# Two layers of a diffusion backbone on one core: expert rows in 8 KB runs, a smaller descriptor memory for GpSimd, one more load tile and two more work tiles

## The chip, the core and the metric

The kernel runs on one core of a Trainium2 chip. Its engines are PE (TensorE: matmuls and their weight loads), DVE (VectorE), ACT (ScalarE), POOL (GpSimd) and SP (SyncE, which here issues loads and stores). Sixteen DMA engines move data between HBM and the core's SBUF, which has 128 partitions. Matmul results land in PSUM. The metric is the device time of one launch in microseconds (us); the kernel before has a median of 1786.24 us over 3 runs (1786.08 to 1787.52).

## The reference

All data are fp32. There are 256 latent tokens and 256 context tokens of width 1024 and two layers; in the second the context tokens are only read. In short:

```python
for l in range(2):
    sh1, sc1, g1, sh2, sc2, g2 = split(silu(c) @ w_mod[l] + b_mod[l])   # and the same for c_ctx
    u = h * (1 + sc1) + sh1
    y = four_mixers_gated_and_projected(u, w_in[l], w_branch[l], w_out[l])
    h = layer_norm(ALPHA * h + g1 * y, ln1)
    u = h * (1 + sc2) + sh2                                # latent and context tokens apart
    aff = softmax(u @ w_router[l])                         # 16 experts
    for e in range(16):                                    # each expert takes its 32 best tokens
        idx = top_k(aff[:, e], 32)
        a, v = u[idx] @ w_gate[l, e], u[idx] @ w_up[l, e]  # 1024 x 1024 each
        out[idx] += aff[idx, e] * ((silu(a) * v) @ w_down[l, e])
    h = layer_norm(ALPHA * h + g2 * out, ln2)
```

One expert has three matrices of 4 MB. Layer 0 runs them for 64 rows (32 latent, 32 context), layer 1 for 32.

## The kernel before

**Stages.** Each layer has the modulation vectors, the projections and mixers (lines to about 860), the routing (`route`, `choose`), and then the experts in order 0 to 15 (`gu0`, `down0` in layer 0 and `gu1`, `down1` in layer 1), each with SwiGLU between the two parts. Tokens of an expert are gathered by a matmul with a one-hot matrix (`gather`, `gather_one`), turned so that the width lies on partitions (transposes of PE against an identity, which put the tile to be turned in the weight load), and modulated into `xs`. In `down0` and `down1` the activations are turned in the same way (L1100, L1127). An expert's matmul then takes 128 indices of the contracted dimension at a time: step `kt` has on partition p the index kt * 128 + p, and the weight tile must hold the same row there.

**Loads of the experts.** `ex_raw` cuts a matrix into four 1 MB parts of 256 rows. A part lies in a tile of [128, 2, 1024]: partition p gets row p and row 128 + p, thus two runs of 4 KB. Where a part goes into a pair of tiles of [128, 1024] (tags `b4`, `p`, `pt`) or four of [128, 512] (`wbs`), `go` issues one load for each tile. The last expert's `w_down` is cut by columns instead, into runs of 1 KB.

**What sets the order of the loads.** The loop at the end of `trunk` issues all loads from SP in the order in which the program needs them, up to `LEAD` = 16 parts ahead. SP works in order: where the next tile is still in use, it and all behind it wait. Which tile a part gets is written in three tables: `early` (tiles that are free while the last mixer runs), `order` (the tiles as they come free at the end of the mixers), and `ring` (the cycle afterwards). Tags: `raw` (4 tiles of 8 KB a partition, also used for all weights of the mixers), `w8` (7), `q8`, `k8`, `cst`, `wbr` (1 each), the pairs and `wbs`. Smaller work tiles (2 KB a partition) have the tag `t2`, 7 of them. PE, DVE and ACT are ordered by the language's scheduler; SP and POOL keep the written order.

**GpSimd's loads.** POOL issues the small ones: `b_mod` (`load_b`), the layer norm vectors (`load_ln`, `ln_rows`), `w_router`, the bias table (L510). A part of SBUF, 16 KB of each partition, is set aside for the descriptors that these loads are made of.

**Where the contracted index order enters.** It is in `modT` and `lnT` (vectors with the width on partitions), in `wr` (the router), in the transposes of `turned` (L902), `gather` (L1010), `gather_one` (L1036), `down0` (L1100) and `down1` (L1127), and, undone, in `g_bcast` (L321, L324), which turns a vector of `modT` into rows.

Of the kernel before, what the change touches and what calls it, by code (L numbers as in the profile page):

```python
# [86 lines left out]
def trunk(ctx: ExitStack, tc: tile.TileContext, x, c, ctx_in, c_ctx, w_mod, b_mod, w_in, qk_gain,  # L87
          sink_logit, na_rpb, w_branch, w_out, ln1_g, ln1_b, w_router, w_gate, w_up, w_down,
          ln2_g, ln2_b, consts, ident_in, out):
    nc = tc.nc  # L90
# [5 lines left out]

    N_RAW, N_W8, N_T2 = 4, 7, 7
    N4 = {"b4": 10, "p": 2, "pt": 2}
# [72 lines left out]
    def load_b(l):  # L171
        bsrc = t2([48, 128])
        G.dma_start(bsrc, b_mod[l].rearrange("(k p) -> k p", p=128))
        p = ps_t([128, 48])
        T.transpose(p, bsrc, ident[0:48, 0:48])
        V.tensor_copy(bT[l], p)

    def load_ln(l):
        lsrc = t2([32, 128])
        for n, v in enumerate((ln1_g, ln1_b, ln2_g, ln2_b)):  # L180
            G.dma_start(lsrc[8 * n:8 * n + 8], v[l].rearrange("(k p) -> k p", p=128))
        p = ps_t([128, 32])
        T.transpose(p, lsrc, ident[0:32, 0:32])
        V.tensor_copy(lnT[l].rearrange("p n k -> p (n k)"), p)

# [57 lines left out]
    def mod_tr(l, group):  # L243

        grp, n = group[0] // 4, len(group)
        step = group[1] - group[0]
        qs = slice(group[0] % 4, group[-1] % 4 + 1, step)
        p = ps_t([128, 4, 8])
        for g in range(4):
            T.matmul(p[:, g], mrows[l, group][:, g * 128:g * 128 + 128], sel[:, 0:8], start=True, stop=True)  # L250
        mt = modT[l][:, 4 * grp:4 * grp + 4][:, qs]
        V.tensor_tensor(mt, p.rearrange("p g (q j) -> p q g j", j=2)[:, qs],
                        bT[l][:, grp * 16:grp * 16 + 16].rearrange("p (q g) -> p q g", g=4)[:, qs].unsqueeze(3)
                        .to_broadcast([128, n, 4, 2]), op=OP.add)
# [60 lines left out]
    def g_bcast(l, m, j, ns=range(2)):  # L315
        t = gbc[l, m, j] if (l, m, j) in gbc else b4([128, D])
        gbc[l, m, j] = t
        for n in ns:
            p = ps_mm()
            for g in range(4):  # L320
                T.matmul(p[:, g * 128:g * 128 + 128],  # L321
                         modT[l][:, 2 * m + n, g, j:j + 1].to_broadcast([128, 128]), ident,
                         start=True, stop=True)
            A.activation(t[:, n * 512:n * 512 + 512], p, AF.Copy)  # L324

# [33 lines left out]
    def ex_raw(l, e, kind, q):  # L359
# [7 lines left out]

        rows = w[l, e, q * 256:q * 256 + 256, :].rearrange("(k p) n -> p k n", p=128)

        def go(t):  # L370
            if isinstance(t, list):
                n = 2 * D // len(t)
                for k in range(len(t)):
                    nc.sync.dma_start(t[k], rows[:, k * n // D, k * n % D:k * n % D + n])
            else:
                nc.sync.dma_start(t, rows)
        return (("ex", l, e, kind, q), [128, 2, D], go)
# [66 lines left out]
    def small_loads(l):  # L444
# [7 lines left out]
        G.memset(wr[:, end:end + 1], 0.0)  # L452
        G.dma_start(wr[:, 0:8], w_router[l].rearrange("(k p) e -> p k e", p=128))
        st_["small"] = {"gq": gq, "snk": snk, "wr": wr}

    def layer(l):
# [440 lines left out]
        def turned(t, hf):  # L897
# [3 lines left out]
            for k in range(4):  # L901
                T.transpose(pt[:, k], st_["h"][t][:, (4 * hf + k) * 128:(4 * hf + k) * 128 + 128], ident)  # L902
            (A.activation(u, pt, AF.Copy) if hf else V.tensor_copy(u, pt))
# [90 lines left out]
        def gather(gr, s, pr):  # L994
# [14 lines left out]
            for q in range(4):  # L1009
                T.transpose(p[:, q].rearrange("p n e c -> p (n e c)"), rows[:, q * 128:q * 128 + 128], ident)  # L1010
            for n in range(2):
# [9 lines left out]
        def gather_one(s, e):  # L1021
# [75 lines left out]
        def down0(e, a):  # L1097
            p = ps_t([128, 4, 128])
            for q in range(4):
                T.transpose(p[:, q], a[:, q * 128:q * 128 + 128], ident)  # L1100
            hT = t2([128, 4, 128])
# [22 lines left out]
        def down1(e, a):  # L1124
            p = ps_t([128, 4, 64])
            for q in range(4):
                T.transpose(p[:, q], a[:, q * 128:q * 128 + 128], ident[0:64, 0:64])  # L1127
            hT = t2([128, 4, 64])
# [539 lines left out]
    def ex_tile(tag, shape):  # L1668
# [6 lines left out]
        if tag == "wbs":  # L1675
# [5 lines left out]
    flat = [(j, r) for j, (fn, rs) in enumerate(events) for r in rs]  # L1681
    order = [["raw"] * 2 + ["wbr", "wbs"] + ["b4"] * 2 + ["raw"] * 2 + ["w8"] * 3 + ["q8", "b4"] + ["w8"] * 4 + ["k8", "cst"]
             + ["raw"] * 2 + ["wbr", "b4", "b4", "raw"],
                    ["b4"] * 2 + ["raw"] * 4 + ["wbs", "wbr"] + ["w8"] * 2 + ["b4"] + ["w8"] * 3 + ["q8"]]
    ring = [["raw"] + ["w8"] * 3 + ["q8"] + ["w8"] * 4 + ["cst"] + ["raw"] * 2 + ["wbr", "raw"],
            ["cst"] + ["w8"] * 2 + ["raw"] * 2 + ["p", "pt"] + ["raw"] * 2 + ["wbr"] + ["w8"] * 5 + ["q8"]]
    early = [deque(["cst"]), deque(["cst", "w8", "w8", "k8", "p", "pt"])]
# [59 lines left out]
```

## Time and profile before

| what | value |
|---|---|
| median of 3 runs | 1786.24 us (1786.08 to 1787.52) |
| the profiled execution | 1786.01 us, of which 1783.9 us from its first to its last instruction |
| PE busy, matmuls | 1556.6 us, 87% |
| DVE, ACT, POOL busy | 39%, 24%, 7% |
| moved by DMA | 533.04 MB in 194120 packets, mean 299 GB/s |
| mean granted TensorE clock | 0.954 |

The kernel is one program with stages of different limits, so the shares above are averages. The stages are told apart by the line of GB/s in 40 slices of 44.6 us each and by windows. A packet is one contiguous run that a DMA engine moves; the count of packets and the MB of a stretch give its mean run. PE's busy time counts from the start of a matmul to its modelled end.

### The profile page before, as it was taken

How to read it: one execution, taken by the hardware profiler on the slowest of the kernel's cores; microseconds unless marked ns; L12 is line 12 of the kernel's file. 1: busy time of each engine (PE TensorE's matmuls, PEld its weight loads, DVE VectorE, ACT ScalarE, POOL GpSimd, SP SyncE). 2: the span in 40 equal slices, each digit the busy share in tenths (PEclk: the TensorE clock that was granted, in tenths of full speed). 3: DMA queues.
4: the chain of work that ended last, by engine and by line, in shares of the span. 5: the costliest groups of instructions: out<-in, count | busy, mean ns of one | idle time of the engine just before them, and what ended most of it. 6: DMA issues, size and time to landing. Idle time of an engine off the chain costs nothing.

```text
span 1783.9 us, 22960 instructions
## 1 busy us (share of the span) xinstructions
PE 1556.6 (87%) x9315; PEld 891.8 (50%) x9315; DVE 700.0 (39%) x1378; ACT 432.7 (24%) x929; POOL 131.6 (7%) x176
## 2 busy tenths in 40 slices
PE   7999999999989989899998899999977666767665
PEld 4777778778854333323332588888832212112112
DVE  3564463663542332222222685857533101112114
ACT  2343433343231010101200454445321001001000
POOL 1200012111010000000000320111100000000000
PEclk9999999999989999999999999999979889888888
DMA  9544354453659999999999665657889999999996
GB/s 310 169 145 175 113 182 109 145 185 122 259 194 375 395 409 409 409 409 409 409 409 400 230 236 174 226 120 262 327 312 408 409 409 409 409 409 409 409 409 243
DMA packets 194120, 533.04 MB, mean 299 GB/s; under 512 B 9520, under 2 KB 61088, under 8 KB 194016
## 3 DMA queue, kind: packets, MB, share of 16 engines
q1 hardware_dynamic: 192016, 527.49, 77.8%
q0 software_dynamic: 1856, 4.02, 1.3%
q8 instruction: 73, 1.20, 0.3%
q14 instruction: 31, 0.25, 0.0%
q10 hardware_dynamic: 144, 0.07, 0.0%
HBM read 530.50 MB, written 1.05 MB: 298 GB/s over the span
## 4 chain that ended last, share of the span: by engine, by line
PE 66%; DMA 15%; issue 11%; DVE 5%; ACT 2%; POOL 1%; SPq 0%; ACTq 0%; DVEq 0%; POOLq 0%
PE mm L769 14%; PE mm L1086 12%; PE mm L531 7%; DMA w<-in_w_up_dram 6%; PE mm L1107 5%; DMA raw<-in_w_up_dram 4%; PE mm L780 3%; PE mm L1120 2%; PE pt L217 2%; PE mm L849 2%; DMA w<-in_w_down_dram 2%; PE ps L1003 2%; PE ps L641 2%; PE pt L722 1%; PE ps L1144 1%
## 5 line engine op out<-in xcount | busy, mean ns | idle before, releaser
L769 PE MATMUL mm<-w,b 128*128 128x512 f32 (+1 forms) x1536 | 291.1, 341 | 0.4 <-DVE b L424 0.4
L769 PEld LDWEIGHTS mm<-w,b 128*128 128x128 f32 x1536 | 238.1, 189 | 46.2 <-issue 15.9
L1075 ACT ACTIVATE t<-mm 128x512 f32<-128x512 f32 (+1 forms) x32 | 19.0, 594 | 666.2 <-PE mm L1120 354.7
L1076 DVE SCALAR_TENSOR_TENSOR t<-t,mm 128x512 f32<-128x512 f32 (+1 forms) x32 | 21.9, 683 | 368.3 <-ACT t L1075 368.3
L424 DVE TENSOR_TENSOR b<-raw,b 128x1024 fp32r<-128x1024 f32 (+1 forms) x95 | 113.2, 1194 | 118.3 <-ACT b L422 113.6
L531 PE MATMUL mm<-b,w 128*128 128x512 f32 (+1 forms) x720 | 148.7, 359 | 5.2 <-ACT b L422 3.6
L531 PEld LDWEIGHTS mm<-b,w 128*128 128x128 f32 x720 | 115.7, 192 | 30.6 <-ACT b L422 4.0
L422 ACT ACTIVATE b<-raw 128x1024 fp32r<-128x1024 f32 (+1 forms) x96 | 97.9, 1021 | 126.0 <-PE mm L769 90.3
L1093 DVE TENSOR_TENSOR k<-mm,b 32x512 f32<-32x512 f32 (+1 forms) x96 | 53.1, 553 | 184.8 <-PE mm L1107 84.7
L1120 PE MATMUL mm<-w,b 128*32 128x512 f32 x416 | 92.3, 725 | 30.5 <-DMA w<-in_w_up_dram 25.6
L1086 PE MATMUL mm<-w,b 128*64 128x512 f32 x480 | 116.9, 596 | 1.9 <-DMA w<-in_w_gate_dram 1.2
L798 POOL TENSOR_TENSOR b<-b,t 128x256 f32<-128x256 f32 x72 | 56.2, 794 | 502.5 <-DVE t L792 485.6
L780 PE MATMUL mm<-w,wbs 128*128 128x512 f32 (+1 forms) x384 | 78.4, 339 | 0.1
L1120 PE MATMUL mm<-raw,b 128*32 128x512 f32 x256 | 49.2, 664 | 31.1 <-DMA raw<-in_w_up_dram 17.4
L1086 PEld LDWEIGHTS mm<-w,b 128*64 128x64 f32 x480 | 37.9, 137 | 70.1 <-issue 63.9
L1086 PE MATMUL mm<-raw,b 128*64 128x512 f32 x280 | 70.9, 594 | 0.7 <-DMA raw<-in_w_gate_dram 0.7
L780 PEld LDWEIGHTS mm<-w,wbs 128*128 128x128 f32 x384 | 61.2, 188 | 8.8 <-ACT w L630 0.3
L1120 PEld LDWEIGHTS mm<-w,b 128*32 128x32 f32 x416 | 17.3, 121 | 93.6 <-DMA w<-in_w_up_dram 45.3
L1107 PE MATMUL mm<-w,t 128*64 128x512 f32 x240 | 59.0, 618 | 2.9 <-ACT t L1102 2.9
L679 ACT ACTIVATE p<-ps,st 128x512 f32<-128x512 f32 (+1 forms) x72 | 43.6, 613 | 52.7 <-DVE st L677 50.3
L1086 PEld LDWEIGHTS mm<-raw,b 128*64 128x64 f32 x280 | 22.0, 137 | 40.8 <-issue 38.9
L1144 PE MATMUL ps<-k,wbs 128*128 128x512 f32 x72 | 38.4, 651 | 4.4 <-DVE k L1093 3.7
(371 smaller groups left out, 2199.0 us busy)
## 6 DMA issues: line engine op xcount, KB each, us to landing
w<-in_w_up_dram SPq DMA_DIRECT2D x64, 1024.0 KB, 18.1
w<-in_w_down_dram SPq DMA_DIRECT2D x59, 1024.0 KB, 17.2
raw<-in_w_mod_dram SPq DMA_DIRECT2D x48, 1024.0 KB, 5.7
w<-in_w_gate_dram SPq DMA_DIRECT2D x48, 1024.0 KB, 18.3
raw<-in_w_in_dram SPq DMA_DIRECT2D x46, 1024.0 KB, 7.1
raw<-in_w_down_dram SPq DMA_DIRECT2D x35, 1024.0 KB, 16.0
raw<-in_w_up_dram SPq DMA_DIRECT2D x34, 1024.0 KB, 15.3
raw<-in_w_gate_dram SPq DMA_DIRECT2D x33, 1024.0 KB, 15.3
```

What stands on the lines that cost most here:

```text
L422: A.activation(hi, src, AF.Copy)
L424: eng.tensor_tensor(lo, src, hi.bitcast(F32), op=OP.subtract)
L531: T.matmul(p, uu(kt, t * 128, t * 128 + 128), ww[:, kt % 2, a:n], start=kt == 0 and i == 0, stop=kt == 7 and i == 2)
L679: A.activation(P[:, hh, a:b], s[:, hh, a:b], AF.Exp, scale=0.125, bias=nm[:, n:n + 1], accum_out=rs[:, n:n + 1])
L769: T.matmul(p, ww[:, kt], uu(kt, 0, NTOK), start=n == 0, stop=n == 23)
L780: T.matmul(p, ww[:, k, o:o + 128], br[i][:, j, k], start=n == 0, stop=n == 5)
L798: G.tensor_tensor(m, m, e[:, c], op=OP.add)
L1086: T.matmul(p[fh * 64:fh * 64 + 64], xs[kt // 4][:, kt % 4, e % 4], ex_w(l, e, kind, kt, fh * 512, 512), start=kt == 0, stop=kt == 7)
L1093: V.tensor_tensor(dst, pd[q], g, op=OP.mult)
L1107: T.matmul(pd[dh * 64:dh * 64 + 64], hT[:, q, fh * 64:fh * 64 + 64], ex_w(l, e, "d", f, dh * 512, 512), start=f == 0, stop=f == 7)
L1120: T.matmul(p[r:r + 32], xs[kt // 4][:, kt % 4, e % 4], ex_w(l, e, kind, kt, fh * 512, 512), start=kt == 0, stop=kt == 7)
L1144: T.matmul(p[:, dh], loc["sm", gr][:, s, t], loc["y", gr][s][:, dh * 512:dh * 512 + 512], start=True, stop=True)
```

## The change

Expert parts are cut so that partition p gets rows 2p and 2p + 1 of the 256, which lie next to each other in HBM: one run of 8 KB. With that the contracted index of step `kt` on partition p becomes 256 * (kt // 2) + 2p + kt % 2, in place of 128 * kt + p. `paired` names these columns, and every place that turns something for the experts or the router reads them with a step of two. For `modT` and `lnT` the vectors of the second half of a layer take the new order and those of the first half the old: `load_b` and `load_ln` therefore turn each vector both ways (`turned_both`, four transposes for one, two copies for one). `g_bcast` writes with a step to put the order back. The router's rows are loaded with the new order too. The memory for GpSimd's descriptors becomes 4 KB of each partition; the 12 KB go to a fifth `raw` tile and two more `t2`.

```diff
-    N_RAW, N_W8, N_T2 = 4, 7, 7
+    N_RAW, N_W8, N_T2 = 5, 7, 9
...
+        bsrc = t2([24, 256])
+        G.dma_start(bsrc, b_mod[l].rearrange("(k p) -> k p", p=256))
+        p = turned_both(bsrc, 24)
+        b = bT[l].rearrange("p (q k) -> p k q", k=2)
+        V.tensor_copy(b[:, :, 0:8], p[:, 0, :, 0:8])
+        V.tensor_copy(b[:, :, 8:24], p[:, 1, :, 8:24])
...
+    def paired(kt):
+        c = kt // 2 * 256 + kt % 2
+        return slice(c, c + 255, 2)
+
+    def turned_both(src, n):
+
+        p = ps_t([128, 2, 2, n])
+        for k in range(2):
+            T.transpose(p[:, 0, k], src[:, k * 128:k * 128 + 128], ident[0:n, 0:n])
+            T.transpose(p[:, 1, k], src[:, k:k + 255:2], ident[0:n, 0:n])
+        return p
...
-            A.activation(t[:, n * 512:n * 512 + 512], p, AF.Copy)
+            A.activation(t[:, n * 512:n * 512 + 512].rearrange("p (q i k) -> p q k i", q=2, k=2),
+                         p.rearrange("p (q k i) -> p q k i", q=2, k=2), AF.Copy)
...
-        rows = w[l, e, q * 256:q * 256 + 256, :].rearrange("(k p) n -> p k n", p=128)
+        rows = w[l, e, q * 256:q * 256 + 256, :].rearrange("(p k) n -> p k n", p=128)
...
-                nc.sync.dma_start(t, rows)
+                nc.sync.dma_start(t.rearrange("p k n -> p (k n)"), rows.rearrange("p k n -> p (k n)"))
...
-        G.dma_start(wr[:, 0:8], w_router[l].rearrange("(k p) e -> p k e", p=128))
+        G.dma_start(wr[:, 0:8].rearrange("p (q k) e -> p q (k e)", k=2),
+                    w_router[l].rearrange("(q p k) e -> p q (k e)", p=128, k=2))
...
-                T.transpose(pt[:, k], st_["h"][t][:, (4 * hf + k) * 128:(4 * hf + k) * 128 + 128], ident)
+                T.transpose(pt[:, k], st_["h"][t][:, paired(4 * hf + k)], ident)
...
-                T.transpose(p[:, q], a[:, q * 128:q * 128 + 128], ident)
+                T.transpose(p[:, q], a[:, paired(q)], ident)
...
-                    ["b4"] * 2 + ["raw"] * 4 + ["wbs", "wbr"] + ["w8"] * 2 + ["b4"] + ["w8"] * 3 + ["q8"]]
+                    ["b4"] * 2 + ["raw"] * 5 + ["wbs", "wbr"] + ["w8"] * 2 + ["b4"] + ["w8"] * 3 + ["q8"]]
...
-            ["cst"] + ["w8"] * 2 + ["raw"] * 2 + ["p", "pt"] + ["raw"] * 2 + ["wbr"] + ["w8"] * 5 + ["q8"]]
+            ["cst"] + ["w8"] * 2 + ["raw"] * 2 + ["p", "pt"] + ["raw"] * 3 + ["wbr"] + ["w8"] * 5 + ["q8"]]
...
-    nc = _bacc.Bacc("TRN2", target_bir_lowering=False, num_devices=1)
+    nc = _bacc.Bacc("TRN2", target_bir_lowering=False, num_devices=1,
+                     dynamic_dma_scratch_size=4096)
```

The loads move in SP's order. The first place is the start of layer 1's experts, where SP fills the tiles that the mixers leave. A row is the line, the tile and its source, and the shape; `b` stands for the tag `b4`, `w` for `w8`, `q` for `q8`. Before:

```order
L376 DMA raw<-in_w_gate_dram 128x2x1024
L376 DMA raw<-in_w_up_dram 128x2x1024
L376 DMA raw<-in_w_down_dram 128x2x1024 x2
L374 DMA wbs<-in_w_gate_dram 128x512 x4
L376 DMA wbr<-in_w_up_dram 128x2x1024
L376 DMA w_9537<-in_w_gate_dram 128x2x1024
```

And in the changed kernel:

```order
L396 DMA raw<-in_w_gate_dram 128x2048
L396 DMA raw<-in_w_up_dram 128x2048
L396 DMA raw<-in_w_down_dram 128x2048 x2
L396 DMA raw<-in_w_gate_dram 128x2048
L394 DMA wbs<-in_w_up_dram 128x512 x4
L396 DMA wbr<-in_w_gate_dram 128x2048
L396 DMA w_9555<-in_w_up_dram 128x2048
```

There are five loads into `raw` in place of four, and the parts behind them take other tiles. A full tile is one row of 2048 elements per partition.

The second place follows shortly after on SP: the last loads up to the one into `cst`, which still holds a part of expert 0. Before:

```order
L376 DMA w_9716<-in_w_up_dram 128x2x1024
L376 DMA w_9718<-in_w_gate_dram 128x2x1024
L376 DMA w_9720<-in_w_up_dram 128x2x1024
L376 DMA q_9722<-in_w_down_dram 128x2x1024
L376 DMA cst<-in_w_down_dram 128x2x1024
```

And in the changed kernel:

```order
L396 DMA w_9734<-in_w_gate_dram 128x2048
L396 DMA w_9736<-in_w_up_dram 128x2048
L396 DMA w_9738<-in_w_down_dram 128x2048
L396 DMA q_9740<-in_w_down_dram 128x2048
L396 DMA cst<-in_w_down_dram 128x2048
```

The same tiles come in the same order up to the load that has to wait; because of the fifth `raw`, one part more lies ahead of it.

The third place is the end of layer 1's loads on SP. Before:

```order
L376 DMA raw<-in_w_gate_dram 128x2x1024
L376 DMA raw<-in_w_up_dram 128x2x1024
L374 DMA p<-in_w_gate_dram 128x1024 x2
L374 DMA pt<-in_w_up_dram 128x1024 x2
L365 DMA raw<-in_w_down_dram 128x8x256 x2
L365 DMA wbr<-in_w_down_dram 128x8x256
L365 DMA w_11551<-in_w_down_dram 128x8x256
```

And in the changed kernel:

```order
L394 DMA pt<-in_w_up_dram 128x1024 x2
L396 DMA raw<-in_w_gate_dram 128x2048
L396 DMA raw<-in_w_up_dram 128x2048
L396 DMA raw<-in_w_gate_dram 128x2048
L396 DMA wbr<-in_w_up_dram 128x2048
L396 DMA w_11553<-in_w_gate_dram 128x2048
L396 DMA w_11555<-in_w_up_dram 128x2048
L385 DMA w_11557<-in_w_down_dram 128x8x256
L385 DMA w_11559<-in_w_down_dram 128x8x256
L385 DMA w_11561<-in_w_down_dram 128x8x256
L385 DMA q_11563<-in_w_down_dram 128x8x256
```

The ring has 17 entries in place of 16. Its `p` and `pt` pairs are still two loads with 4 KB for a partition, and the last matrix, in runs of 1 KB, goes into other tiles. PE, DVE and ACT have nearly the same order as before.

## Rows read from the trace of the kernel before

**Rows 1.** The page's slices: PE's busy tenths and GB/s, 40 slices.
```profile
PE   7999999999989989899998899999977666767665
...
GB/s 310 169 145 175 113 182 109 145 185 122 259 194 375 395 409 409 409 409 409 409 409 400 230 236 174 226 120 262 327 312 408 409 409 409 409 409 409 409 409 243
```

**Rows 2.** Windows by stage: length, busy us (instructions) PE, PEld, DVE, ACT, POOL; clock, DMA share, GB/s.
```profile
50.00:480.00 430.00, 427.12 (x2329) 329.64 (x2328) 224.90 (x431) 165.16 (x352) 57.37 (x75) 1.00 0.46 154
...
540.00:920.00 380.00, 354.34 (x1642) 132.23 (x1640) 106.57 (x198) 48.28 (x116) 2.93 (x8) 0.99 1.01 403
920.00:960.00 40.00, 33.17 (x145) 9.74 (x141) 7.59 (x11) 2.62 (x5) 0.00 (x0) 1.00 1.03 409
...
1310.70:1317.70 7.00, 6.19 (x34) 1.55 (x30) 1.26 (x5) 1.47 (x5) 0.00 (x0) 0.50 0.00 1
1317.80:1756.00 438.20, 307.21 (x2252) 94.31 (x2244) 77.03 (x156) 31.59 (x79) 3.57 (x6) 0.89 1.03 408
```

**Rows 3.** The chain of waits from 1317.8 to 1756 us, shares by line.
```profile
by line: issue 38.5%; DMA w<-in_w_up_dram 23.5%; DMA raw<-in_w_up_dram 16.9%; DMA w<-in_w_down_dram 7.5%; PE mm L1120 7.4%; PE mm L1134 3.3%; PE ps L1003 1.4%; DVE t L1077 0.8%; ACT t L1075 0.7%; DVE t L1076 0.6%; PE pt L1010 0.6%; PE pt L1
```

**Rows 4.** DMA packet counts from 24 to 28, 42.3 to 44, 1317.8 to 1756 us.
```profile
DMA packets 1376, 1.39 MB, mean 348 GB/s; under 512 B 16, under 2 KB 1376, under 8 KB 1376
...
DMA packets 91, 0.71 MB, mean 420 GB/s; under 512 B 1, under 2 KB 1, under 8 KB 91
...
DMA packets 47422, 178.62 MB, mean 408 GB/s; under 512 B 3096, under 2 KB 4135, under 8 KB 47399
```

**Rows 5.** Timeline of SP, 36 to 42 us: start, us, line, load.
```profile
37.89 0.57 SPq L143 DMA_DIRECT2D cst<-in_consts_dram  x1
```

**Rows 6.** DMA queue of SP's loads, 1317.8 to 1756 us: packets, MB, share.
```profile
q1 hardware_dynamic: 47111, 177.24, 101.7%
```

**Rows 7.** DMA issues, 1317.8 to 1756 us: count, size, median us to landing.
```profile
p<-in_w_gate_dram SPq DMA_DIRECT2D x16, 512.0 KB, 16.8
...
pt<-in_w_down_dram SPq DMA_DIRECT2D x6, 512.0 KB, 16.0
b<-in_ln_g_dram SPq DMA_DIRECT2D x1, 512.0 KB, 13.4
```

**Rows 8.** Timeline of SP around 1300 us.
```profile
1296.98 0.98 SPq L376 DMA_DIRECT2D q<-in_w_down_dram  x1
1316.80 0.37 SPq L376 DMA_DIRECT2D cst<-in_w_down_dram  x1
```

**Rows 9.** PE's waits for loads, 480 to 1000 us: total us, times, longest.
```profile
PE mm L1086 <- DMA w<-in_w_gate_dram: 1.2, 2, 0.6
...
PE mm L1086 <- DMA raw<-in_w_gate_dram: 0.7, 1, 0.7
PE mm L1107 <- DMA raw<-in_w_down_dram: 0.7, 1, 0.7
PE mm L1086 <- DMA w<-in_w_up_dram: 0.6, 1, 0.6
PE mm L1086 <- DMA cst<-in_w_up_dram: 0.6, 1, 0.6
```

**Rows 10.** Weight loads of the transposes in layer 0: ns min/median/max, first and last start.
```profile
L1100 PEld LDWEIGHTS pt<-idsel,t x60: 138/140/231, 545.7 to 948.8; 128*128 128x128 f32 x60
...
L1010 PEld LDWEIGHTS pt<-idsel,t x56: 137/140/143, 571.5 to 860.6; 128*128 128x128 f32 x56
...
L1036 PEld LDWEIGHTS mm<-idsel,t x8: 137/139/183, 523.0 to 546.5; 128*128 128x128 f32 x8
...
L902 PEld LDWEIGHTS pt<-idsel,p x16: 138/141/196, 483.2 to 504.9; 128*128 128x128 f32 x16
```

**Rows 11.** GpSimd's loads of the bias table, and the matmuls that use them.
```profile
277.38 5.34 POOL L510 DMA_DIRECT2D t<-in_na_rpb_dram  x8
...
DMA to landing us min/median/max: 4.8/6.5/10.5
...
L513 PE MATMUL pt<-t,cst x16: 483/486/590, 297.6 to 1179.2; 128*128 128x384 f32 x16
```

More of the change, by code (lines that the diff above doesn't have):

```diff
@@ L171, in load_b @@
     def load_b(l):
[L172 to L176, printed above, removed]
+        bsrc = t2([24, 256])
[4 more added lines that the diff above has]
+        V.tensor_copy(b[:, :, 8:24], p[:, 1, :, 8:24])
     def load_ln(l):
-        lsrc = t2([32, 128])
+        lsrc = t2([16, 256])
         for n, v in enumerate((ln1_g, ln1_b, ln2_g, ln2_b)):
[L181 to L184, printed above, removed]
+            G.dma_start(lsrc[4 * n:4 * n + 4], v[l].rearrange("(k p) -> k p", p=256))
+        p = turned_both(lsrc, 16)
+        b = lnT[l].rearrange("p n (q k) -> p k (n q)", k=2)
+        V.tensor_copy(b[:, :, 0:8], p[:, 1, :, 0:8])
+        V.tensor_copy(b[:, :, 8:16], p[:, 0, :, 8:16])
     def silu_c():
@@ L249, in mod_tr @@
         for g in range(4):
-            T.matmul(p[:, g], mrows[l, group][:, g * 128:g * 128 + 128], sel[:, 0:8], start=True, stop=True)
+            c = paired(g) if group[0] > 3 else slice(g * 128, g * 128 + 128)
+            T.matmul(p[:, g], mrows[l, group][:, c], sel[:, 0:8], start=True, stop=True)
         mt = modT[l][:, 4 * grp:4 * grp + 4][:, qs]
@@ L1009, in gather @@
             for q in range(4):
-                T.transpose(p[:, q].rearrange("p n e c -> p (n e c)"), rows[:, q * 128:q * 128 + 128], ident)
+                T.transpose(p[:, q].rearrange("p n e c -> p (n e c)"), rows[:, paired(q)], ident)
             for n in range(2):
@@ L1035, in gather_one @@
             for k in range(2):
-                T.transpose(p[:, k].rearrange("p q c -> p (q c)"), rows[:, k * 128:k * 128 + 128], ident)
+                T.transpose(p[:, k].rearrange("p q c -> p (q c)"), rows[:, paired(k)], ident)
             for kt in range(8):
@@ L1126, in down1 @@
             for q in range(4):
-                T.transpose(p[:, q], a[:, q * 128:q * 128 + 128], ident[0:64, 0:64])
+                T.transpose(p[:, q], a[:, paired(q)], ident[0:64, 0:64])
             hT = t2([128, 4, 64])
@@ L1681, in trunk @@
     flat = [(j, r) for j, (fn, rs) in enumerate(events) for r in rs]
-    order = [["raw"] * 2 + ["wbr", "wbs"] + ["b4"] * 2 + ["raw"] * 2 + ["w8"] * 3 + ["q8", "b4"] + ["w8"] * 4 + ["k8", "cst"]
+    order = [["raw"] * 2 + ["wbr", "wbs"] + ["b4"] * 2 + ["raw"] * 3 + ["w8"] * 3 + ["q8", "b4"] + ["w8"] * 4 + ["k8", "cst"]
              + ["raw"] * 2 + ["wbr", "b4", "b4", "raw"],
-                    ["b4"] * 2 + ["raw"] * 4 + ["wbs", "wbr"] + ["w8"] * 2 + ["b4"] + ["w8"] * 3 + ["q8"]]
-    ring = [["raw"] + ["w8"] * 3 + ["q8"] + ["w8"] * 4 + ["cst"] + ["raw"] * 2 + ["wbr", "raw"],
-            ["cst"] + ["w8"] * 2 + ["raw"] * 2 + ["p", "pt"] + ["raw"] * 2 + ["wbr"] + ["w8"] * 5 + ["q8"]]
+                    ["b4"] * 2 + ["raw"] * 5 + ["wbs", "wbr"] + ["w8"] * 2 + ["b4"] + ["w8"] * 3 + ["q8"]]
+    ring = [["raw"] * 2 + ["w8"] * 3 + ["q8"] + ["w8"] * 4 + ["cst"] + ["raw"] * 2 + ["wbr", "raw"],
+            ["cst"] + ["w8"] * 2 + ["raw"] * 2 + ["p", "pt"] + ["raw"] * 3 + ["wbr"] + ["w8"] * 5 + ["q8"]]
     early = [deque(["cst"]), deque(["cst", "w8", "w8", "k8", "p", "pt"])]
```

## The prediction

> **What bounds the kernel now.** I read the line of transferred GB/s over the 40 slices first. It has two plateaus of 409 GB/s, slices 15 to 21 and 32 to 39 [rows 1]: the experts of layer 0 and of layer 1. Everywhere else the rate swings between 109 and 395. The windows by stage [rows 2] then say which engine is full in each. In the projections and mixers of layer 0 (50 to 480 us) PE is busy 427.1 of 430 us, so loads hardly matter there. In the experts of layer 0 (540 to 920 us) PE is busy 354.3 of 380 us with the DMA engines full beside it: nearly balanced, PE ahead. From 920 to 960 PE falls to 33.2 of 40. In the experts of layer 1 (1317.8 to 1756 us) PE is busy only 307.2 of 438.2 us while the DMA share is 1.03 at 408 GB/s: this stage lasts as long as its bytes take. The chain of waits of that stretch agrees: the largest parts that name something are loads of `w_up` and `w_down`, and PE's expert line L1120 has 7.4% of it [rows 3]. So a change of the transfer rate counts in full in layer 1, and in layer 0 only where PE waits for a load.
>
> **Part 1: 8 KB runs, layer 1.** What a longer run is worth must come from rows with other run lengths. The packet counts give three [rows 4]: 1376 packets of 1 KB moved at 348 GB/s, the 4 KB packets of the stage at 408 to 409, and 91 packets of 0.71 MB, 7.9 KB each, at 420. The last are rows of the constants table, the one load with 7936 bytes in a row (128x1984 fp32, issued at 37.89 us [rows 5]); one packet each, so a run over 4 KB is not cut. As time of one packet on one of 16 engines that is 16 x 1024 / 348 = 47.1 ns and 16 x 4096 / 409 = 160.2 ns: 36.8 ns for each 1000 bytes and 9.4 ns whatever the length. Continued to 8192 bytes this gives 311.0 ns, 421 GB/s; the 7936-byte row, not used in the line, has 420 where the line says 421. I take 421.
>
> How many bytes get it: the first queue moves 177.24 MB in the stage [rows 6]. Of these, 44 half tiles of 0.524 MB (names `p` and `pt`, first and last of four groups [rows 7]) are loaded as one 4 KB row per partition and stay so; behind the start of the stage the changed order has 40 of them, 21.0 MB. The layer norm rows (1.05 MB on this queue, one of two shown [rows 7]) and the 1 KB runs of the last matrix (4135 packets under 2 KB less 3096 under 512 B, 1.06 MB [rows 4]) stay too. One tile goes away to part 2 (1.05 MB). That leaves 177.24 - 21.0 - 1.05 - 1.06 - 1.05 = 153.1 MB in 8 KB runs: 374.3 us at 409, 363.7 us at 421. **Minus 10.7 us**, all on the path, since PE has 131 us to spare. The bounds: no time lost per packet at all would be 16 / 0.0368 = 435 GB/s, 352.2 us, minus 22; no rise of the rate would be 0. Below that, a loss, I have no row to exclude: nothing in the trace reads HBM with an 8 KB pitch between partitions. Both neighbours (409 at a 4 KB pitch, 420 at 8.6 KB) speak against it.
>
> The Trainium skill's page "DMA: Bandwidth & Descriptors", section "Why small descriptors are slow (HBM only)", puts the loss per packet at about 3 cycles beside one cycle for each 32 bytes. By that rule 4 KB would cost 131 cycles and 8 KB 259 instead of 262, and the rate would be 414, not 421. This case's trace disagrees so far: by the same rule 1 KB packets would run at 383 GB/s, and they run at 348.
>
> **Part 2: one more tile for loads.** Before layer 1's first expert the loader fills every free tile, then waits. SP issued the load into `q` at 1296.98 us and the next, into `cst`, at 1316.80 [rows 8]; from 1310.7 to 1317.7 nothing was moved [rows 2]. The wait ends when L1120 has used the first tile of expert 0, which is also so in the changed order, but with one more `raw` load ahead of the wait. The 7 us hole holds 1.05 MB easily, and these bytes need not be moved in the full stage: 1.05 / 0.409 = **minus 2.6 us**. In layer 0 the fifth tile helps where PE waits for loads, which is counted next; in the projections PE has 2.9 us of idle time in 430 to give, and none of it I count.
>
> **Part 3: 8 KB runs and the tile, layer 0.** PE is the slower side until about 920 us; then the stock is used up, and PE waits for five groups of expert loads for 1.2 + 0.7 + 0.7 + 0.6 + 0.6 = 3.8 us [rows 9]. With 421 for 409 the loader gains 2.9% of 380 us, 11 us, before that point, so these waits go: **minus 3.8 us**. What is late next is PE itself (L1086, L1107), so no more follows; bounds 0 and 6.8, all of PE's idle time from 920 to 960 [rows 2].
>
> **Part 4: what the new row order costs.** The hidden index is now taken in pairs, so the transposes ahead of an expert read their 128 columns with a step of two. PE issues the same instructions in nearly the same order, and the step is in the weight load. In layer 0, where PE bounds, these are 60 (L1100), 56 (L1010), 8 (L1036) and 32 (L902, two names of 16) [rows 10]: 156 loads of 140 ns. No row has a weight load with a step of two. I take 0; from the other side, a doubled load is 156 x 0.140 = 21.8 us, since four such transposes follow each other at about the load's own 140 ns. In layer 1 they lie beside waits for DMA.
>
> On this the Trainium skill's page "SBUF — State Buffer" (the paragraph on cachelines under the DMA port swizzle) says that fp32 may be read at a step of up to four elements at full speed. By it the term is 0, by the bound above 21.8; no run here shows which yet.
>
> The three extra transposes of each small load (`load_b`, `load_ln`), the second copy beside each, the strided write of `g_bcast` and the changed `w_router` load I cost at nothing: the first `load_b` lies ahead of PE's wait for the first weights, the others are a few PE instructions of 0.14 us, under 2 us if all were on the path. GpSimd's smaller descriptor memory could delay its loads. The nearest are the eight loads of the bias table, issued from 277.38 us, landing after 6.5 us and used from 297.6 [rows 11]: 20 us of cover, so 0; one after another they would take 8 x 6.5 = 52 us, 32 more than the cover, in each layer, so a serial queue would cost some 60. Against that stands that eight loads issued within 5.34 us land after 4.8 to 10.5 us each, so they overlap now. The two work tiles I count at 0: PE's waits in the experts are for data.
>
> **Sum.** The profiled execution took 1786.01 us (span 1783.9), 0.2 under the median of 1786.24. 1786.0 - 10.7 - 2.6 - 3.8 = **1768.9 us**, 1.0% less.
>
> **The rivals.**
> *The rate hardly rises.* The 420 is a mean over 1.7 us and may flatter; halfway between the rows at 4 KB and 7.9 KB lies 414.5. Then 153.1 MB take 369.4 us, minus 4.9; with parts 2 and 3, 1786.0 - 11.3 = 1774.7. For it the short stretch; against it that the 348 at 1 KB, over 4 us, leads to the same 421. The rule of the Trainium skill's DMA page above would give 414, and so this case.
> *The rate does not rise at all*, because HBM and not the packet sets the 409: part 2 alone, 1783.4, no change that could be told. For it that 409 is so constant; against it the 420.
> *Slower: the stepped weight load.* If each of the 156 transposes of layer 0 takes its 140 ns twice, PE, which bounds there, is 21.8 us longer, and layer 0's gain is gone too: 1786.0 + 21.8 - 10.7 - 2.6 = 1794.5. It decides from about 85 ns more per load (13.3 / 156). For it that these loads set the pace of a transpose; against it that the transposes are 4 to 8 in a row behind a wait, and only 156 among some thousands of PE's instructions of the stage.
> *Faster still*: packets overlap and the rate nears 435, or the earlier loads and work tiles take more of layer 0's idle time: 1786.0 - 22 - 2.6 - 6.8 = 1754.6 at the end.
>
> **Chances and range.** About 0.2% (3.6 us) is what a measurement of this kernel can tell from no change. Forecast (1764 to 1773) 0.62; rate hardly rises 0.13; not at all 0.07; slower 0.07; faster still 0.11. The range goes down to between the forecast and the fastest case and up past the small rise, to 1760 to 1779; left out are the slow case, no rise, and about half of the fastest. Faster by over 0.2%: 0.62 + 0.13 + 0.11 = 0.86; within 0.2% 0.07; slower 0.07.
>
> **What would show it.** In the changed profile: about half as many packets on the first queue (each expert tile 128 of 8192 bytes); plateaus of 419 to 423 GB/s in both expert stages; the layer 1 stage of full transfers about 425 instead of 438 us; no PE waits for DMA in layer 0's experts and PE over 93% busy to their end; the weight loads of the transposes still at 140 ns. Plateaus at 414 or 409 would make the first or second rival right, loads of 200 ns and more the slow one; a gap of GpSimd's loads ahead of L513 would be something I priced at nothing.

## The result and the profile after

The changed kernel takes 1775.45 us (median of 4 runs, 1775.23 to 1775.93) against 1786.16 us for the kernel before on the same chip: ratio 0.9945, 95% interval 0.9929 to 0.9961. The gain is 10.7 us where the forecast's terms add up to 17.1. The profiled execution has a span of 1772.9 us, 11.0 less than before.

The page's slices of the changed kernel, PE and GB/s, answer to [rows 1]:

```profile
PE   7999999999989989899999899999978766667665
...
GB/s 341 164 144 179 122 177 111 143 214 95 253 182 398 346 411 422 420 421 421 422 421 403 203 210 214 201 117 250 297 331 403 420 419 419 419 420 419 419 420 234
```

Both plateaus have risen from 409 to between 419 and 422. The windows by stage (columns as in [rows 2]) say what became of it:

```profile
540.00:920.00 380.00, 352.90 (x1622) 133.91 (x1618) 106.51 (x198) 47.97 (x115) 3.12 (x8) 0.99 0.99 408
920.00:960.00 40.00, 36.33 (x166) 12.35 (x163) 8.73 (x12) 3.71 (x7) 0.00 (x0) 1.00 1.01 422
1310.50:1317.60 7.10, 5.92 (x34) 1.50 (x30) 1.25 (x5) 1.47 (x5) 0.00 (x0) 0.50 0.00 0
1317.70:1743.70 426.00, 306.13 (x2244) 97.98 (x2236) 77.03 (x156) 31.39 (x79) 3.68 (x6) 0.89 1.01 417
1743.70:1755.10 11.40, 8.16 (x52) 2.93 (x52) 2.76 (x5) 1.48 (x4) 0.00 (x0) 0.70 0.87 281
1755.10:1772.90 17.80, 4.44 (x45) 2.50 (x44) 11.04 (x19) 1.94 (x4) 3.57 (x3) 0.68 0.16 59
```

The last two stretches, the 1 KB runs of the last matrix and what follows them, were these in the kernel before:

```profile
1756.00:1767.50 11.50, 7.74 (x68) 3.47 (x64) 3.67 (x7) 2.07 (x5) 0.00 (x0) 0.85 0.83 272
1767.50:1783.90 16.40, 2.70 (x24) 1.62 (x24) 10.24 (x17) 1.35 (x3) 3.58 (x3) 0.65 0.17 64
```

So the span splits like this (us):

| piece | before | after | difference | forecast |
|---|---|---|---|---|
| up to the first full load of layer 1's experts | 1317.8 | 1317.7 | -0.1 | -3.8 |
| full loads of layer 1 | 438.2 | 426.0 | -12.2 | -13.3 |
| 1 KB runs of the last matrix | 11.5 | 11.4 | -0.1 | 0 |
| from there to the end | 16.4 | 17.8 | +1.4 | 0 |

Layer 1 gave nearly what it should. Layer 0 gave nothing, and the end lost something: of what is missing, 3.7 us lie in layer 0, 1.1 in the full loads and 1.3 at the end. The weight loads of the transposes in layer 0 of the changed kernel (min/median/max in ns, first and last start), for [rows 10]:

```profile
L1121 PEld LDWEIGHTS pt<-idsel,t x60: 194/209/230, 544.6 to 948.7; 128*128 128x128 f32 x60
...
L1031 PEld LDWEIGHTS pt<-idsel,t x56: 194/209/223, 572.2 to 863.9; 128*128 128x128 f32 x56
...
L1057 PEld LDWEIGHTS mm<-idsel,t x8: 195/200/223, 522.0 to 545.9; 128*128 128x128 f32 x8
...
L923 PEld LDWEIGHTS pt<-idsel,p x16: 195/209/234, 481.6 to 503.7; 128*128 128x128 f32 x16
```

They rose from 140 to 209 ns: 156 x 0.069 = 10.8 us if none of it were covered. PE's longest waits from 480 to 1000 us (total us, times, longest) are now these, and the view lists no load, where [rows 9] had five groups of them:

```profile
PE pt L1031 <- DVE t L1027: 11.3, 12, 2.9
PE mm L1128 <- ACT t L1123: 8.6, 11, 1.4
PE pt L1121 <- DVE t L1098: 4.7, 6, 0.8
```

So 3.8 us of waits went away in layer 0, and something as large came in their place. For the full loads of layer 1, the packets and the queue of SP's loads, for [rows 4, 6]:

```profile
DMA packets 28357, 177.49 MB, mean 417 GB/s; under 512 B 3047, under 2 KB 4015, under 8 KB 9647
...
q1 hardware_dynamic: 28046, 176.11, 100.4%
```

The queue has 28046 packets for 47111, and 1.1 MB fewer to move in this stage. The gap ahead of it is as long as it was (7.1 us), so that megabyte moved before it.

### The profile page after: what moved, and what is told of

Its sections match the earlier page's. It is cut to its first block, busy times and chain, and to the rows that moved or that the text cites. A ratio compares the mean times of both kernels' runs of the same rounds, so it can differ in the third digit from the quotient of the medians.

```text
span 1772.9 us, 22976 instructions
## 1 busy us (share of the span) xinstructions
PE 1561.2 (88%) x9327; PEld 903.0 (51%) x9327; DVE 699.7 (39%) x1382; ACT 432.6 (24%) x929; POOL 132.8 (7%) x176
## 4 chain that ended last, share of the span: by engine, by line
PE 67%; DMA 15%; issue 10%; DVE 5%; ACT 2%; POOL 1%; SPq 0%; DVEq 0%; ACTq 0%; POOLq 0%
PE mm L790 15%; PE mm L1107 13%; PE mm L552 7%; PE mm L1128 6%; DMA w<-in_w_down_dram 4%; PE mm L801 4%; DMA raw<-in_w_up_dram 3%; DMA w<-in_w_up_dram 2%; PE pt L235 2%; PE mm L870 2%; PE ps L662 2%; PE ps L1024 2%; PE pt L743 1%; PE ps L1165 1%; PE ps L861 1%
## 5 line engine op out<-in xcount | busy, mean ns | idle before, releaser
L819 POOL TENSOR_TENSOR b<-b,t 128x256 f32<-128x256 f32 x72 | 60.5, 854 | 499.7 <-DVE t L813 475.4
L1141 PE MATMUL mm<-raw,b 128*32 128x512 f32 x296 | 59.0, 644 | 17.0 <-DMA raw<-in_w_up_dram 12.1
L1128 PE MATMUL mm<-w,t 128*64 128x512 f32 x216 | 51.8, 614 | 2.9 <-ACT t L1123 2.9
L1128 PE MATMUL mm<-raw,t 128*64 128x512 f32 x168 | 40.1, 597 | 2.9 <-ACT t L1123 2.9
```

The lines of the kernel that those rows point to most:

```text
L819: G.tensor_tensor(m, m, e[:, c], op=OP.add)
L1128: T.matmul(pd[dh * 64:dh * 64 + 64], hT[:, q, fh * 64:fh * 64 + 64], ex_w(l, e, "d", f, dh * 512, 512), start=f == 0, stop=f == 7)
L1141: T.matmul(p[r:r + 32], xs[kt // 4][:, kt % 4, e % 4], ex_w(l, e, kind, kt, fh * 512, 512), start=kt == 0, stop=kt == 7)
```

## The experiments

**Theory A**: what is missing went to the stepped weight loads of layer 0, which read every second column. **Rivals**: the memory part costs it (B); layer 0's gain is lost in the mixers that follow (C); three came with later runs (E: TensorE bounds the last 25 us; F: layer 0's loads are hidden anyway; G: weight loads are covered). Ratios are to the kernel before on the same chip, with 95% intervals. "Start" is when the first full load of layer 1's experts moves, "full" how long the 4 and 8 KB packets last from there, "rest" the time from the last of them to the end, all in us of the profiled execution, worked out from its packets.

| kernel | median | ratio | start | full | rest |
|---|---|---|---|---|---|
| before | 1785.05 to 1786.16 | 1 | 1317.8 | 438.1 | 27.9 |
| after | 1775.45 | 0.9945 (0.9929 to 0.9961) | 1317.7 | 426.0 | 29.3 |
| after_again | 1775.79 | 0.9949 (0.9937 to 0.9961) | 1319.2 | 426.1 | 28.8 |
| step_only | 1788.23 | 1.0015 (1.0003 to 1.0027) | 1318.9 | 437.8 | 27.8 |
| mem_only | 1782.08 | 0.9982 (0.9973 to 0.9992) | 1316.9 | 435.9 | 27.7 |
| scratch_only | 1785.83 | 1.0001 (0.9991 to 1.0010) | 1315.2 | 437.5 | 27.8 |
| runs_only | 1775.21 | 0.9942 (0.9930 to 0.9953) | 1317.8 | 428.8 | 27.8 |
| l0_only | 1784.70 | 1.0000 (0.9990 to 1.0010) | 1320.4 | 434.9 | 29.0 |
| l1_only | 1772.52 | 0.9932 (0.9919 to 0.9945) | 1316.3 | 425.4 | 27.5 |
| runs_nostep | 1770.10 | 0.9919 (0.9904 to 0.9934) | 1315.3 | 425.4 | 27.7 |
| unstep | 1795.84 | 1.0062 (1.0050 to 1.0074) | 1341.7 | 427.8 | 29.3 |
| step4 | 1794.58 | 1.0057 (1.0043 to 1.0072) | 1323.7 | 438.0 | 27.8 |
| moving | 1784.73 | 1.0001 (0.9990 to 1.0011) | 1328.1 | 426.4 | 27.3 |

The column "full" is the steadiest: 437.5 to 438.1 in four kernels with 4 KB runs and four tiles. "Start" differs by 2.6 us among the four kernels with 4 KB runs and no steps in layer 0, so a single start tells little.

**step_only**, the stepped columns alone, in the kernel before:

```diff
-                T.transpose(p[:, q], a[:, q * 128:q * 128 + 128], ident)
+                T.transpose(p[:, q], a[:, paired(q)], ident)
... the same in turned, gather, gather_one and down1
```

> The kernel before, with the transposes of the hidden vectors (routing, gather, down) reading every second column as the changed kernel does, and nothing else changed: 4 KB runs, four load tiles, the old descriptor memory. The hidden columns then meet weight rows of another index, so the output is not the reference's; the instructions, bytes and shapes are those of before. Theory A (the missing 6.4 us of the gain go to the stepped weight loads of layer 0, which TensorE bounds): weight loads of the transposes 209 ns against 140 ns, 156 of them in layer 0 on TensorE's path, so +4 to +11 us, 1790 to 1797 us. Theory B (the loss comes from GpSimd's smaller descriptor memory or from the other order of tiles, not from the step): 1786 us, within 1 us of before, whatever the weight loads take. Theory C (what layer 0 gains is lost again in the mixers that follow): also 1786 us, since the layer-0 end may move by a few us without the end of the kernel following.

The weight loads of `down0` in this kernel:

```profile
L1104 PEld LDWEIGHTS pt<-idsel,t x60: 194/209/230, 544.6 to 950.1; 128*128 128x128 f32 x60
```

The time rose by 0.15%, 2.7 us (0.5 to 4.8). The step costs time by itself, as A says and B and C do not; but the middle of the interval lies below the 4 us that A had as its lower bound, and its lower end is not clear of the 1 us that B and C left open.

**mem_only** and **scratch_only**, the memory part, whole and without its tiles:

```diff
-    N_RAW, N_W8, N_T2 = 4, 7, 7
+    N_RAW, N_W8, N_T2 = 5, 7, 9
... the tables order and ring with one raw more; scratch_only leaves these out
-    nc = _bacc.Bacc("TRN2", target_bir_lowering=False, num_devices=1)
+    nc = _bacc.Bacc("TRN2", target_bir_lowering=False, num_devices=1,
+                     dynamic_dma_scratch_size=4096)
```

> The kernel before, with the memory part of the change alone: descriptor memory of 4 KB, the fifth load tile with its place in the tables of tiles, nine work tiles; runs stay at 4 KB. By the prediction's term (5.5 us more loads in flight over the gap, at the old rate) this gives -2.6 us: 1783.5 us. Theory A: that, between -2 and -4 us. Theory B (the memory part costs what is missing): it gives 0 to +4 us, 1786 to 1790 us.

> The kernel before with the descriptor memory of GpSimd at 4 KB per partition and nothing else. Theory A: no change, within 0.5 us of 1786.2 us, the GpSimd transfers taking the same 4.8 to 10.5 us from issue to landing. Theory B: GpSimd waits for room in the smaller memory before its transfers, and the time rises by 2 to 6 us.

mem_only gained 0.18%, 3.2 us (1.4 to 4.8), and scratch_only changed nothing. The bias table's loads of scratch_only, for [rows 11]:

```profile
DMA to landing us min/median/max: 4.7/6.4/10.0
```

B is out: the smaller descriptor memory costs nothing that can be seen, and the fifth tile earns about what it was priced at (full: 438.1 to 435.9, 2.2 us for 2.6).

**runs_only**, the changed kernel without its memory part (the edit above undone).

> The changed kernel with the memory part undone: runs of 8 KB and stepped transposes, but four load tiles, the old tables of tiles, seven work tiles and the old descriptor memory. Theory A (rate term right, stepped weight loads eat layer 0): what the change gave, 10.7 us, less the 2.6 us of the fifth tile: about 1778 us. Theory B (the memory part takes 6.4 us instead of giving 2.6): 1769 to 1770 us, faster than the changed kernel.

It took 1775.21 us, as fast as the changed kernel: neither number came. The full loads show the tile at work here too, 428.8 us without it and 426.0 with it. But the changed kernel's rest is 1 to 1.5 us longer, and its start is no earlier, so little of the 2.8 us reaches the end. By the column "full" the 8 KB runs alone gave 438.1 - 428.8 = 9.3 us. The rates in 40 slices of that stage, first mem_only (4 KB), then runs_only (8 KB):

```profile
GB/s 386 395 395 413 409 410 409 408 410 409 409 410 407 409 410 409 409 409 409 409 409 409 411 407 410 407 409 409 410 409 409 409 408 410 410 408 409 409 409 385
```

```profile
GB/s 402 327 421 422 423 413 417 423 420 413 425 420 418 421 422 420 415 420 421 423 412 424 422 420 417 421 420 418 418 420 422 417 422 421 420 414 422 421 421 394
```

409 became about 420 from the third slice on. The second slice shows why the runs gave 9.3 and not 10.7 us: 327 where mem_only has 395, which is 2.4 us lost against 0.4. SP, which issues the loads in order, waits there for PE ahead of a pair of tiles, in the kernel before as in runs_only (from 1317 to 1345 us):

```profile
SPq L374 <- PE mm L1134: 6.3, 2, 5.9
```

```profile
SPq L394 <- PE mm L1155: 7.0, 2, 6.6
```

The wait is nearly the same, but at the higher rate the loads in flight run out in it: in slices of 0.7 us the rate falls to 129 GB/s in runs_only and to 345 in the kernel before.

**after_again**, **l1_only** and **l0_only**: the changed kernel itself beside one that has the runs and steps in layer 1 alone, and one that has them in layer 0 alone:

```diff
-    def paired(kt):
+    def paired(kt, l):
+        if l == 0:                      # l == 1 in l0_only
+            return slice(kt * 128, kt * 128 + 128)
...
-        rows = w[l, e, q * 256:q * 256 + 256, :].rearrange("(p k) n -> p k n", p=128)
+        rows = w[l, e, q * 256:q * 256 + 256, :].rearrange("(p k) n -> p k n" if l else "(k p) n -> p k n", p=128)
```

> The changed kernel itself, to stand on the same chip beside the three kernels after it. Theory A and all others: 1775 us, ratio 0.994 to 0.995. If its ratio is that of the changed kernel without its memory part (0.9942), the fifth tile gives nothing once the runs are 8 KB; if theory A's sum holds it is 0.0015 lower (2.6 us).

> The changed kernel with layer 0 as before: 4 KB runs and contiguous transposes there, 8 KB runs and stepped transposes in layer 1 alone, the memory part kept. Theory A: layer 0 is bound by TensorE, so 8 KB runs give it up to 3.8 us and the steps take 2.7 to 6 us from it: 0 to 3 us faster than the changed kernel, 1772 to 1775 us. If the runs of layer 0 earned their predicted 3.8 us and the steps cost only 2.7: 1776.5 us, 1 us slower.

> The changed kernel with layer 1 as before: 8 KB runs and stepped transposes in layer 0 alone, the memory part kept. By the prediction's terms: -3.8 us for layer 0 and -2.6 us for the fifth tile, 1779.8 us. Theory A (the steps cost what the runs give in layer 0): the fifth tile's gain alone, 1782 to 1784 us, the 0.9982 of the memory part by itself.

l1_only is 3.3 us faster than the changed kernel beside it (1771.02 to 1774.49 against 1774.64 to 1777.29), just past the upper end of what A expected; l0_only, with the fifth tile's gain in it, is no faster than before, 3.2 us behind mem_only and slower than the 1782 to 1784 us of A. So the change is a loss in layer 0 by both ways of asking. Some 1.3 to 1.8 us of each difference lie in the column "rest"; by "start" alone the loss is 1.4 to 2.9 us and 3.5 us. PE's waits for loads in layer 0 of l1_only show what the 8 KB runs could have taken away there:

```profile
PE mm L1115 <- DMA w<-in_w_gate_dram: 0.7, 1, 0.7
...
PE mm L1115 <- DMA wbr<-in_w_up_dram: 0.6, 1, 0.6
PE mm L1136 <- DMA w<-in_w_down_dram: 0.6, 1, 0.6
PE mm L1115 <- DMA raw<-in_w_gate_dram: 0.6, 1, 0.6
```

2.5 us here, 3.8 in the profile of before. l1_only beats both kernels: of those that compute the reference it is the version to keep.

**runs_nostep**, the changed kernel with contiguous columns (the edit of step_only the other way round).

> The changed kernel with contiguous columns in all five transposes, so 8 KB runs and the memory part without the steps; hidden columns then meet weight rows of another index, and the output is not the reference's. What is known by now: loads of layer 1's experts span 426 us in the changed kernel as against 438, and they begin at 1317.7 to 1319.2 us with steps in layer 0 and at 1315.2 to 1317.8 us without. Theory A (the steps take in layer 0 what the runs give there): weight loads at 140 ns, layer 1's bulk of loads from 1315 us, and 3 to 4 us faster than the changed kernel, 1772 us. If the runs of layer 0 earn the whole predicted 3.8 us beside that: 1770 us, faster than the kernel with layer 0 as before (1772.5). Theory F (layer 0's loads are hidden anyway, whatever the steps cost): 1772.5 us, level with that kernel.

It took 1770.10 us, 5.7 less than the changed kernel by the medians and 5.3 by the ratios (0.9919 / 0.9949 = 0.9970, by the two intervals some 2 to 9 us). Its weight loads, and its windows of the full loads, the 1 KB runs and the end:

```profile
L1121 PEld LDWEIGHTS pt<-idsel,t x60: 138/140/230, 545.8 to 947.6; 128*128 128x128 f32 x60
```

```profile
1315.30:1740.70 425.40, 299.34 (x2240) 92.67 (x2232) 77.04 (x156) 31.67 (x79) 3.68 (x6) 0.90 1.01 417
1740.70:1752.20 11.50, 8.18 (x72) 3.83 (x72) 3.67 (x7) 1.81 (x4) 0.00 (x0) 0.85 0.86 279
1752.20:1768.30 16.10, 2.76 (x25) 1.62 (x24) 10.14 (x17) 1.61 (x3) 3.57 (x3) 0.66 0.17 65
```

The start is 2.4 and 3.9 us earlier than in the two profiles of the changed kernel, the full loads are 0.6 to 0.7 shorter, and the rest 1.1 to 1.6. Only the first of these is what A named. How much of the 10.8 us PE has to wait out can be read from single groups of four transposes, one of gather and one of `down0` (start, length in us, what PE waited for before it), here and then in the changed kernel:

```profile
602.48 0.91 PE L1031 MATMUL pt<-idsel,t 128*128 128x128 f32 x4 [0.53 <-DVE t L1027]
691.24 0.66 PE L1121 MATMUL pt<-idsel,t 128*128 128x128 f32 x4 [0.78 <-DVE t L1098]
```

```profile
601.86 0.98 PE L1031 MATMUL pt<-idsel,t 128*128 128x128 f32 x4 [0.53 <-DVE t L1027]
691.10 0.75 PE L1121 MATMUL pt<-idsel,t 128*128 128x128 f32 x4 [0.78 <-DVE t L1098]
```

Four loads are 0.28 us longer, but the group only 0.07 to 0.09. For 156 transposes, 39 such groups, that is an estimate of 2.7 to 3.5 us: the 2.7 of step_only, and the earlier start here. So A holds for some 3 of the 6.4 us that were missing, and G is right about the larger part of the longer loads.

The time lies 2.4 us below l1_only. That would be what 8 KB runs earn in layer 0 when nothing is paid for them, but the intervals of the two overlap and the starts differ by 1.0 us, so this figure is not sure and F is not excluded.

The two windows at the end also show what the end lost: in the changed kernel 45 matmuls still had to run after the last packet, here 25, and the granted clock during the 1 KB runs was 0.70 against 0.85 (1 is 2.4 GHz, 0.5 is 1.2). A rest of 29 us stands in the three profiles with all the steps in layer 0 and the fifth tile together (after, after_again, l0_only) and in unstep; the others have 27.3 to 27.9. The clock goes with it in all 13 traces: between the last 4 or 8 KB packet and PE's last matmul it was at 1.2 GHz for 6.8 us in these four, for 3.4 us in eight others, and not at all in moving, which has the shortest rest. Why it falls just there was not settled, so whether the change or chance put the 1.4 us there stays open. E is not it: l1_only and runs_nostep have the same loads and no such end, and l0_only has the old loads and such an end.

**unstep**: the changed kernel with the permuting moved to VectorE's and ScalarE's copies.

```diff
-            V.scalar_tensor_tensor(a, a, 0.5, pu, op0=OP.mult, op1=OP.mult)
-            return a
+            b = t2([n, 512])
+            V.tensor_tensor(b.rearrange("p (q k i) -> p q i k", q=2, k=2),
+                            a.rearrange("p (q i k) -> p q i k", q=2, k=2),
+                            pu.rearrange("p (q i k) -> p q i k", q=2, k=2), op=OP.mult)
+            return b
... 0.5 goes to the copy of hT; gather's two copies write rows in the same order
```

> The changed kernel with the permuting of the hidden vectors moved from TensorE's weight loads to VectorE and ScalarE, which write it while they copy; gather and down transposes read contiguous columns again (the 48 routing transposes stay stepped). The last multiplication of the activation goes to a second work tile. Theory A (stepped weight loads cost what is missing): weight loads of these transposes back at 140 ns, 4 to 6 us faster than the changed kernel, 1769 to 1771 us. What the stepped loads alone cost in the kernel before was 0.15% (0.03 to 0.27%), 2.7 us; if that is all that they cost here, 1772 to 1773 us. Theory C (layer 0's gain is lost before layer 1's experts begin) and theory E (TensorE bounds the last 25 us of layer 1 once the loads are faster): within 1 us of the changed kernel.

It lost 20 us to the changed kernel (its profile shows its slowest execution, 1800.61 us, so the start in the table is late by up to 5 us). The groups of VectorE from 600 to 920 us (busy us, mean ns), first unstep, then after_again:

```profile
L1106 DVE TENSOR_TENSOR t<-t,mm 128x512 f32<-128x512 f32 x10 | 10.4, 1043 | 2.6 <-PE mm L1117 2.3
...
L1029 DVE COPY t<-ps 128x256 f32<-128x256 f32 x12 | 7.2, 597 | 10.6 <-PE ps L1024 10.6
```

```profile
L1098 DVE SCALAR_TENSOR_TENSOR t<-t,mm 128x512 f32<-128x512 f32 x11 | 7.5, 686 | 8.4 <-PE mm L1107 4.6 <-PE ps L1024 3.7
L1027 DVE COPY t<-ps 128x256 f32<-128x256 f32 x12 | 5.1, 423 | 6.3 <-PE ps L1024 6.3
```

And PE waits for just these, in the waits of unstep from 527 to 1018 us:

```profile
PE pt L1033 <- DVE t L1029: 15.7, 13, 3.4
PE pt L1131 <- DVE t L1106: 8.2, 6, 1.8
```

The two lines stood at 11.4 and 4.7 us in after_again. Loads of 140 ns came back, but PE waits for VectorE before each group of transposes, and that work became 0.17 to 0.36 us longer. PE's idle time in layer 0's experts (527 to 1018 us, in after_again 528.5 to 997) rose by 12.8 us. Its busy time rose by 9.7, and TensorE had 1.2 GHz there for 34.8 us against 10.2. The 1769 to 1771 us of A did not come, but the run says nothing against it: it adds costs of its own, and shows that the permuting is on the path wherever it is put between PE's steps.

**step4**: the kernel before with every fourth column.

```diff
-                T.transpose(p[:, q], a[:, q * 128:q * 128 + 128], ident)
+                T.transpose(p[:, q], a[:, q:512:4], ident)
... the same in turned, gather and down1; every second column in gather_one
```

> The kernel before with every fourth column in the transposes of routing, gather and down (every second in the 12 of gather_one), instead of contiguous ones; the output is not the reference's, since columns meet weight rows of another index. Theory A (a weight load takes longer the wider its columns stand apart): loads well over the 209 ns of the step of two, by a straight line (70 ns for each step) 350 ns, and three times the 2.7 us that the step of two cost, about 8 us: 1793 us. Rival (a step has one price, whatever its size): 209 ns and 1788 us, as with the step of two. Theory G (the cost of weight loads is covered in the queue of TensorE, and the 2.7 us were chance): 1785 us.

```profile
L1100 PEld LDWEIGHTS pt<-idsel,t x60: 195/209/230, 546.1 to 954.4; 128*128 128x128 f32 x60
```

The weight load takes 209 ns, as with a step of two: here A's straight line was wrong and the rival right. The time still rose as A had it (9.5 us), for another reason, which a wait of this kernel shows, with that of before under it:

```profile
PE pt L1010 <- ACT t L1007: 17.7, 14, 2.6
```

```profile
PE pt L1010 <- DVE t L1006: 10.0, 12, 2.1
```

Every fourth column lies in both halves of the gathered rows, so the first transpose waits for ScalarE's half too. With the 1.2 us that PE waited for L1007 in the kernel before, the wait became 6.5 us longer, most of the 9.5. The price of the step can't be read from this run's time.

**moving**: the step in the moving operand of the matmuls that write the columns.

```diff
+        def cols(e, w):
+            return w if e == NE - 1 else w.rearrange("p (q i k) -> p q k i", q=2, k=2)
...
-                                 ex_w(l, e, kind, kt, fh * 512, 512), start=kt == 0, stop=kt == 7)
+                                 cols(e, ex_w(l, e, kind, kt, fh * 512, 512)), start=kt == 0, stop=kt == 7)
... the same view of h in gather and gather_one; the transposes of gather and down read contiguous columns
```

> The changed kernel with the step moved from the transposes' weight loads to the moving operand of the matmuls that write those columns: gate and up matmuls read their 512 weight columns in the order even, odd (in two halves), gathers read the rows of h so; the transposes of gather and down read contiguous columns, those of routing stay stepped. The result is the reference's. Theory A: transposes' weight loads back at 140 ns; if a moving operand with a step of two fp32 costs nothing, 1771 to 1773 us, as fast as the kernel with layer 0 as before or faster. If a stepped moving operand is slower like the weight loads (+50%), the 1024 gate and up matmuls of layer 0 at 593 ns would cost 100 us or more: over 1870 us.

PE's groups in layer 0, first moving, then after_again:

```profile
L1111 PE MATMUL mm<-w,b 128*64 128x512 f32 x456 | 118.5, 612 | 0.0
...
L1024 PE MATMUL ps<-p,t 128*64 128x512 f32 x56 | 23.4, 685 | 0.0
```

```profile
L1107 PE MATMUL mm<-w,b 128*64 128x512 f32 x456 | 114.6, 594 | 0.0
...
L1024 PE MATMUL ps<-p,t 128*64 128x512 f32 x56 | 21.4, 618 | 0.0
```

Neither case came: a matmul is 18 ns longer, 3%. With 1024 of them in layer 0, two side by side, that is 1024 / 2 x 0.018 = 9.2 us. The kernel to set beside it is runs_nostep, whose transposes of gather and down read contiguous columns too: the start is 12.8 us later than there (8.9 to 10.4 later than in the changed kernel, which pays for the step). What the gathers add to the 9.2, and what the clock does, was not taken apart. The cost per instruction is small, but there are far more of them than of transposes.

## Why the prediction was right, and where its steps were off

The direction and the range were right; the sum was 6.5 us too deep, and the time lies outside the 1764 to 1773 us of the forecast's own case. That it fell near the 1774.7 us of the rival "the rate hardly rises" is chance: the rate did rise.

*Part 1, the rate.* Forecast 409 to 421 and -10.7 us. The plateaus came to 419 to 420 in layer 1 and 420 to 422 in layer 0, and the runs alone gave 9.3 us. "All on the path" was not quite so: at the start of the stage the loads in flight ran out while SP waited for a tile. The line through the packets of 1 KB and 4 KB [rows 4] carried. (The packets fell to 60% and not to half, as the 40 half tiles and the short runs would have told.) The Trainium skill, "DMA: Bandwidth & Descriptors", section "Why small descriptors are slow (HBM only)", gave 414 as an estimate from its loss of about 3 cycles per packet; the traces, with 419 to 422, do not agree. The first two rivals are out.

*Part 2, the fifth tile.* Forecast -2.6; the full loads became 2.2 us shorter with 4 KB runs and 2.8 with 8 KB. Right as a mechanism. In the changed kernel the end became 1.4 us longer, which no step had; that goes with a lower clock there, and l1_only has the fifth tile without it.

*Part 3, layer 0's waits for loads.* Forecast -3.8. The waits did go, all of them, but layer 1's loads did not start earlier (1317.8 before, 1317.7 and 1319.2 after): the stepped weight loads took most of the time (2.7 to 3.5 us by the groups of four). PE was busy 36.3 of the 40 us to 960, 91%, where over 93 was named as a sign.

*Part 4, the step, is the step that failed.* "I take 0" was wrong: 209 ns against 140, one of the prediction's own signs of the slow case, and 2.7 us in the kernel before, 2.4 to 3.9 at the start of layer 1 in the changed one. The bound of 21.8 supposed a load twice as long with nothing beside it; the load became half as long again, and of those 10.8 us about 70% are covered, since a group of four transposes grew by 0.07 to 0.09 us and not by 0.28. So the slow rival had the right mechanism at a price below its own point of decision of 13.3 us. The Trainium skill, "SBUF — State Buffer", the paragraph on cachelines (fp32 at full speed up to a step of four), also made the term 0. For weight loads the traces do not agree with it: 209 ns at a step of two and of four, 140 without.

Of the other items at 0, one was measured: GpSimd's loads land after 4.7 to 11.0 us (median 6.4) in the changed kernel. The extra transposes and copies and the two work tiles were not measured apart; runs_nostep, which has them all, lies 1.2 us above the sum, so together they can't cost much unless a gain elsewhere hides it.

## What to carry to other kernels

Longer runs pay in the stage that lasts as long as its bytes, and a line through the times of packets of two sizes in the same trace priced them well here. What the longer run asks of the other engines (here another order of columns) is paid wherever they are the bound, so such a change should be made only in the stages bound by loads: l1_only is 3 us faster than the change in both layers. Nor was the longer instruction paid in full: a group of four grew by 0.07 to 0.09 us where its loads grew by 0.28, so the length of a whole group is the row to price it from. Before an access pattern that no row shows is costed at nothing, the count of instructions times a plausible rise should stand in the sum and not only among the bounds.

## What the hardware showed that was not expected

A weight load of 128x128 fp32 took 209 ns with a step of two columns and 209 with a step of four, against 140 contiguous: one price for any step that was tried. About 70% of the rise was covered: a group of four transposes grew from 0.66 to 0.75 us. The moving operand in the order even, odd cost 3% (594 to 612 ns) where the weight load cost 49%. At the end of layer 1 the granted clock during the last 11.4 us of loads was 0.70 in the changed kernel and 0.85 in runs_nostep, which has the same loads and the same number of matmuls; in all 13 traces an end of about 29 us goes with 6.8 us at 1.2 GHz before PE's last matmul, a shorter one with 3.4 us or none. What makes the clock fall there stays open.
